# Opening loads on two DMA queues: x on GpSimd's, the weights of block 0 on SP's

## The chip, the cores and the metric

The kernel runs on one core of a Trainium2 chip. The metric is the device time of one execution in microseconds (us). The core has TensorE (PE in the profile; PEld is its weight load), VectorE (DVE), ScalarE (ACT), GpSimd (POOL) and SyncE (SP). SP and GpSimd each have a DMA queue here; both are served by the core's 16 DMA engines.

## What is computed

One decoder block on x of 256 tokens by 1024 channels, float32: an RMS norm, one input projection to 9216 columns, two branches (a gated linear recurrence and a block-sparse attention), a gated sum, an output projection and a SwiGLU network. Cut to its frame:

```python
h = rmsnorm(x, attn_norm_g[l])
proj = h @ w_in[l]
hq, hf, hi, hg, aq, ak, av, gl = jnp.split(proj, IN_SPLITS, axis=-1)
y_hg = hgrn2_mix(hq, hf, hi, hg, lb_all[l], hg_out_norm_g[l]) @ w_branch_hg[l]
...
merged = gates[:, :, 0, :] * y_hg + gates[:, :, 1, :] * y_at
x = x + merged @ w_out[l]
h2 = rmsnorm(x, ffn_norm_g[l])
x = x + (jax.nn.silu(h2 @ w_ffn_gate[l]) * (h2 @ w_ffn_up[l])) @ w_ffn_down[l]
```

## The kernel before

Every matrix product runs on TensorE in a two-part number format: a float32 operand is split into a rounded high part and the low rest, and a product takes three matmuls (high by high, high by low, low by high). The split of weights is the helper `split` (lines 55 and 56): ACT makes the high part, DVE the low part.

The kernel is written with a tile framework that keeps each engine's work in an order chosen at build time by a planner with modelled durations, and sets the waits. An engine executes its own instructions strictly in that order.

The opening, lines 116 to 155, computes block 0 of the projection, that is the first 512 columns of `hi` (columns 2048 to 2559 of `w_in`), into the two PSUM banks `V0`. The 1024 channels are 8 k-tiles of 128. For a k-tile it needs a slice of x (transposed, 128 partitions by 256 tokens, tile `xTr`) and a slice of the weights (128 by 512, tile `raw`, shown as `wraw`). ACT multiplies x by the norm gain, a column of the small tile `vec`, and makes the high part `x_hi` (line 143); DVE makes the low part `x_lo` (line 144); both go to the tiles `XT`, which all later blocks of the projection use as well. ACT and DVE split the weights, and PE makes six matmuls per k-tile, three for each half of the tokens (lines 152 to 154).

The loads come in pieces of k-tiles 0, 1, 2 and 3, 4 and 5, 6 and 7. A k-tile of x is 128 KB, one of the weights 256 KB; `vec` is 17.5 KB. All are issued by SP, in the order x piece, weights piece, and `vec` after the first x piece:

```python
for n in pieces:
    ks = slice(k0, k0 + n)
    xs = slice(4 * g + k0, 4 * g + k0 + n)
    nc.sync.dma_start(xTr[:, xs, :], xT[:, xs, :])
    if g == 0 and k0 == 0:
        nc.sync.dma_start(vec, vecs)
    nc.sync.dma_start(raw[:, ks, :], ...)
```

The weight tiles come from a pool of three buffers (`wp`), shared with all later blocks. After block 0 the kernel starts `feat_block` for the forget gate (F0, matmuls on lines 98, 99 and 101), whose weights SP loads through `load_w` (line 64), then the load of x by tokens (`xtok`, line 206) and the next blocks. GpSimd makes constants at the start (`ones_r`, the identity `ident`, the masks: lines 158 to 172); its first DMA is that of line 258, followed by three loads of a bias table from device memory (line 264).

Of the kernel before, what the change touches and what calls it, by code (L numbers as in the profile page):

```python
# [14 lines left out]
P = 128  # L15
# [12 lines left out]
def tile_hgrn2_moba_block(ctx: ExitStack, tc: tile.TileContext, xm, xT, vecs, table, onehot,  # L28
                          w_in, w_hg, w_at, w_out, w_gate, w_up, w_down, out):
    nc = tc.nc  # L30
# [7 lines left out]
    def pw(name="pw"):  # L38
        return psum.tile([P, 512], F32, name=name, tag="pw", bufs=4)
# [11 lines left out]
    def part(pair, k, m):  # L51
        return pair[k // 4][:, k % 4, m, :]

    def split(src, hi, lo):
        nc.scalar.copy(hi, src)  # L55
        nc.vector.tensor_sub(lo, src, hi.bitcast(F32))  # L56
# [68 lines left out]
    xTr = big.tile([P, KT, S], F32, name="xTr", tag="T1")  # L125
    XT = [big.tile([P, 4, 2, S], F32R, name=f"XT{i}", tag=("XH", "XL")[i]) for i in range(2)]
    V = big.tile([P, 2, D], F32, name="V", tag="T6")
    V0 = [pw(), pw()]
    for g, pieces in enumerate(((1, 1, 2), (2, 2))):
        raw = wp.tile([P, 4, 512], F32, name="wraw")  # L130
        wh = wp.tile([P, 4, 512], F32R, name="whi")
        wl = wp.tile([P, 4, 512], F32R, name="wlo")
        k0 = 0
        for n in pieces:
            ks = slice(k0, k0 + n)
            xs = slice(4 * g + k0, 4 * g + k0 + n)
            nc.sync.dma_start(xTr[:, xs, :], xT[:, xs, :])
            if g == 0 and k0 == 0:
                nc.sync.dma_start(vec, vecs)
            nc.sync.dma_start(raw[:, ks, :], w_in[xs.start * P:xs.stop * P, 2048:2560].rearrange("(k p) c -> p k c", p=P))  # L140
            for kt in range(xs.start, xs.stop):
                x_hi, x_lo = part(XT, kt, 0), part(XT, kt, 1)
                nc.scalar.mul(x_hi, xTr[:, kt, :], vec[:, kt:kt + 1])
                nc.vector.scalar_tensor_tensor(x_lo, xTr[:, kt, :], vec[:, kt:kt + 1], x_hi.bitcast(F32),
                                               op0=OP.mult, op1=OP.subtract)
                if kt == xs.start:
                    split(raw[:, ks, :], wh[:, ks, :], wl[:, ks, :])
            for i in range(k0, k0 + n):
                kt = 4 * g + i
                for tb in range(2):  # L150
                    ts = slice(tb * P, (tb + 1) * P)
                    nc.tensor.matmul(V0[tb], part(XT, kt, 0)[:, ts], wh[:, i, :], start=(kt == 0), stop=False)
                    nc.tensor.matmul(V0[tb], part(XT, kt, 1)[:, ts], wh[:, i, :], start=False, stop=False)
                    nc.tensor.matmul(V0[tb], part(XT, kt, 0)[:, ts], wl[:, i, :], start=False, stop=(kt == KT - 1))
            k0 += n
# [7 lines left out]
    for j in range(7):  # L163
        c = 1 << j
# [54 lines left out]
    def put_tok(dst, ps, half):  # L219
        for tb in range(2):  # L220
            nc.scalar.mul(dst[:, tb, half * 512:(half + 1) * 512], ps[tb], rx[:, tb:tb + 1])

    put_tok(V, V0, 0)

# [313 lines left out]
    for half in range(2):  # L538
# [9 lines left out]
        for j in range(2):  # L548
            ks = slice(half * 4 + 2 * j, half * 4 + 2 * j + 2)
# [10 lines left out]
    for half in range(2):  # L560
        ps = tok_block(w_out, half * 512, M)
        for tb in range(2):
            xs = x2[:, tb, half * 512:(half + 1) * 512]
# [112 lines left out]
```

## Time and profile before

| | |
|---|---|
| median of 3 runs | 513.78 us (513.46 to 514.15) |
| the profiled execution, its time | 513.5 us |
| the profiled execution, its span (first to last instruction) | 511.4 us |
| PE busy | 502.2 us, 98% of the span |
| DVE, ACT, POOL busy | 69%, 57%, 5% of the span |
| granted TensorE clock, mean | 1.000 |

The span leaves out 2.1 us around the program. Matmul durations overlap their neighbours, so a busy PE is not one at its peak; how far apart matmuls start tells its pace. In a timeline row the bracket at the end is the idle time of that engine just before the row, and what ended it. SPq is SP's DMA queue: a row of it is the issue of a DMA, not the transfer.

### The profile page before, as it was taken

The page shows a single profiled execution, that of the slowest core. Times are in us where ns is not written, and L with a number is a line of the kernel's source. Part 1 is how long each engine was busy: PE and PEld are TensorE (multiplying, and loading weights), DVE is VectorE, ACT ScalarE, POOL GpSimd, SP SyncE. Part 2 cuts the span into 40 slices and gives each one's busy share as a digit, 9 for nine tenths or more (in the row PEclk, how much of TensorE's full clock was granted, in tenths as well). Part 3 has the DMA queues.
Part 4 walks back from the last instruction along what each step waited for, and adds up shares of the span by engine and source line. Part 5 has one row for each costly group of instructions (what it writes and reads, how often), then busy time and mean ns, then how long its engine had stood idle before and what let it go on. Part 6 is the DMA issues. An engine that isn't in the chain of part 4 may idle for free.

```text
span 511.4 us, 6690 instructions
## 1 busy us (share of the span) xinstructions
PE 502.2 (98%) x2674; PEld 427.5 (84%) x2674; DVE 350.9 (69%) x406; ACT 291.8 (57%) x447; POOL 25.4 (5%) x42
## 2 busy tenths in 40 slices
PE   6999999999999999999999999999999999999996
PEld 5878878788888888988888888888888888888885
DVE  4769998977597663297667777767665646657372
ACT  5597538776639644975554464665634535444250
POOL 8002340000000000000000000000000000000000
PEclk9999999999999999999999999999999999999999
DMA  7956955725422743256665456555655565553522
GB/s 234 390 197 182 347 178 168 243 82 166 164 84 82 247 142 106 83 171 242 190 213 173 166 181 229 165 164 172 208 198 164 186 226 165 177 193 86 181 105 82
DMA packets 43806, 91.20 MB, mean 178 GB/s; under 512 B 1880, under 2 KB 4472, under 8 KB 43776
## 3 DMA queue, kind: packets, MB, share of 16 engines
q1 hardware_dynamic: 43040, 88.14, 51.8%
q0 software_dynamic: 736, 2.65, 1.7%
q8 instruction: 21, 0.34, 0.3%
q14 instruction: 9, 0.07, 0.0%
HBM read 89.70 MB, written 1.07 MB: 178 GB/s over the span
## 4 chain that ended last, share of the span: by engine, by line
PE 86%; DVE 6%; ACT 3%; DMA 1%; POOL 1%; issue 1%; SPq 0%; DVEq 0%; POOLq 0%
PE pw L99 30%; PE pw L98 13%; PE pw L83 6%; PE pw L81 6%; PE pw L82 6%; PE acc L598 4%; PE acc L596 4%; PE acc L597 4%; DVE wlo L56 3%; PE ph L320 2%; PE pw L101 2%; ACT whi L55 2%; DMA wraw<-w_in 1%; POOL qk L295 1%; PE pa L437 1%
## 5 line engine op out<-in xcount | busy, mean ns | idle before, releaser
L56 DVE TENSOR_TENSOR wlo<-wraw,whi 128x2048 fp32r<-128x2048 f32 (+2 forms) x88 | 190.8, 2169 | 105.4 <-ACT whi L55 105.0
L55 ACT CAST whi<-wraw 128x2048 fp32r<-128x2048 f32 (+2 forms) x88 | 156.0, 1774 | 104.4 <-issue 29.5
L99 PE MATMUL pw<-x2T,whi 128*128 128x512 f32 x352 | 121.8, 398 | 0.0
L99 PE MATMUL pw<-XT,whi 128*128 128x512 f32 x256 | 89.6, 399 | 0.0
L98 PE MATMUL pw<-x2T,wlo 128*128 128x256 f32 x308 | 86.6, 281 | 0.0
L99 PEld LDWEIGHTS pw<-x2T,whi 128*128 128x128 f32 x352 | 63.5, 188 | 12.3
L98 PE MATMUL pw<-XT,wlo 128*128 128x256 f32 x224 | 62.8, 281 | 0.0
L98 PEld LDWEIGHTS pw<-x2T,wlo 128*128 128x128 f32 x308 | 58.3, 189 | 1.8
L81 PE MATMUL pw<-whi,XT 128*128 128x512 f32 x144 | 56.9, 395 | 0.8 <-DVE Q L111 0.8
L82 PE MATMUL pw<-wlo,XT 128*128 128x512 f32 x144 | 56.8, 394 | 0.0
L83 PE MATMUL pw<-whi,XT 128*128 128x512 f32 x144 | 56.5, 392 | 0.0
L99 PEld LDWEIGHTS pw<-XT,whi 128*128 128x128 f32 x256 | 46.5, 188 | 9.9 <-ACT Fg L110 0.4
L98 PEld LDWEIGHTS pw<-XT,wlo 128*128 128x128 f32 x224 | 42.4, 189 | 1.4
L596 PE MATMUL acc<-whi,hT 128*128 128x512 f32 x88 | 34.3, 390 | 0.0
L598 PE MATMUL acc<-whi,hT 128*128 128x512 f32 x88 | 34.3, 390 | 0.0
L597 PE MATMUL acc<-wlo,hT 128*128 128x512 f32 x88 | 34.3, 389 | 0.0
L81 PEld LDWEIGHTS pw<-whi,XT 128*128 128x128 f32 x144 | 27.1, 188 | 6.5 <-DVE Q L111 1.1
L83 PEld LDWEIGHTS pw<-whi,XT 128*128 128x128 f32 x144 | 27.0, 188 | 5.6
L82 PEld LDWEIGHTS pw<-wlo,XT 128*128 128x128 f32 x144 | 27.1, 188 | 5.5 <-DVE wlo L56 0.3
L110 ACT COPY fl<-pw 128x256 f32<-128x256 f32 x38 | 14.0, 370 | 24.9 <-PE pw L99 24.9
L99 PE MATMUL pw<-aT,whi 128*128 128x512 f32 x64 | 22.3, 397 | 0.0
L99 PE MATMUL pw<-oT,whi 128*128 128x512 f32 x64 | 22.3, 397 | 0.0
(209 smaller groups left out, 708.4 us busy)
## 6 DMA issues: line engine op xcount, KB each, us to landing
wraw<-w_in SPq DMA_DIRECT2D x32, 1024.0 KB, 5.2
wraw<-w_down SPq DMA_DIRECT2D x11, 1024.0 KB, 4.8
wraw<-w_gate SPq DMA_DIRECT2D x10, 1024.0 KB, 5.0
wraw<-w_up SPq DMA_DIRECT2D x10, 1024.0 KB, 5.0
wraw<-w_at SPq DMA_DIRECT2D x4, 1024.0 KB, 4.9
wraw<-w_hg SPq DMA_DIRECT2D x4, 1024.0 KB, 5.0
wraw<-w_out SPq DMA_DIRECT2D x4, 1024.0 KB, 5.0
wraw<-w_in SPq DMA_DIRECT2D x7, 512.0 KB, 8.8
```

Of the source, the lines that this page charges most:

```text
L55: nc.scalar.copy(hi, src)
L56: nc.vector.tensor_sub(lo, src, hi.bitcast(F32))
L81: nc.tensor.matmul(ps[tb], part(act, kt, 0)[:, ts], wh, start=(kt == 0), stop=False)
L82: nc.tensor.matmul(ps[tb], part(act, kt, 0)[:, ts], wl, start=False, stop=False)
L83: nc.tensor.matmul(ps[tb], part(act, kt, 1)[:, ts], wh, start=False, stop=(kt == KT - 1))
L98: nc.tensor.matmul(ps[ct][:, 0:S], lo[:, i, cs], part(act, kt, 0), start=False, stop=False)
L99: nc.tensor.matmul(ps[ct], hi[:, i, cs], both, start=(kt == 0), stop=(kt == KT - 1))
L101: nc.tensor.matmul(ps[ct][:, 0:S], lo[:, i, cs], part(act, kt, 0), start=False, stop=False)
L110: nc.scalar.copy(dst, hi)
L596: nc.tensor.matmul(acc[tb][half], act[:, j, 0, ts], hi[:, i, cs], start=st, stop=False)
L597: nc.tensor.matmul(acc[tb][half], act[:, j, 0, ts], lo[:, i, cs], start=False, stop=False)
L598: nc.tensor.matmul(acc[tb][half], act[:, j, 1, ts], hi[:, i, cs], start=False, stop=en)
```

## The change

SP issues x of k-tile 0 first. GpSimd's queue gets the other k-tiles of x in three DMAs (k-tile 1, 2 and 3, 4 to 7), ahead of its constants. In the loop SP issues only the weights, and `vec` after the weights of k-tile 0.

```diff
     V0 = [pw(), pw()]
+    nc.sync.dma_start(xTr[:, 0:1, :], xT[:, 0:1, :])
+    for k0, k1 in ((1, 2), (2, 4), (4, 8)):
+        nc.gpsimd.dma_start(xTr[:, k0:k1, :], xT[:, k0:k1, :])
     for g, pieces in enumerate(((1, 1, 2), (2, 2))):
         raw = wp.tile([P, 4, 512], F32, name="wraw")
...
         for n in pieces:
             ks = slice(k0, k0 + n)
             xs = slice(4 * g + k0, 4 * g + k0 + n)
-            nc.sync.dma_start(xTr[:, xs, :], xT[:, xs, :])
+            nc.sync.dma_start(raw[:, ks, :], w_in[xs.start * P:xs.stop * P, 2048:2560].rearrange("(k p) c -> p k c", p=P))
             if g == 0 and k0 == 0:
                 nc.sync.dma_start(vec, vecs)
-            nc.sync.dma_start(raw[:, ks, :], w_in[xs.start * P:xs.stop * P, 2048:2560].rearrange("(k p) c -> p k c", p=P))
```

## Rows read from the trace of the kernel before

**Rows 1.** The page: span, and median landing of the 1024 KB loads of w_in.

```profile
span 511.4 us, 6690 instructions
...
wraw<-w_in SPq DMA_DIRECT2D x32, 1024.0 KB, 5.2
```

**Rows 2.** Busy time by stage, sum over 13 to 490 us (four stages).

```profile
sum 477.00, PE 475.84 PEld 406.48 DVE 335.13 ACT 281.77 POOL 14.50; mean PE 118.96 PEld 101.62 DVE 83.78 ACT 70.44 POOL 3.63
```

**Rows 3.** Timeline of PE in block 0: start, duration, line; the last is F0's first.

```profile
5.32 0.79 PE L152 MATMUL pw<-whi,XT 128*128 128x512 f32 x1 [0.42 <-ACT whi L55]
...
9.33 0.40 PE L154 MATMUL pw<-wlo,XT 128*128 128x512 f32 x1
12.14 0.49 PE L152 MATMUL pw<-whi,XT 128*128 128x512 f32 x1 [2.41 <-ACT whi L55]
...
20.83 0.39 PE L99 MATMUL pw<-XT,whi 128*128 128x512 f32 x1
```

**Rows 4.** Timeline of ACT: the split of the weights of k-tiles 2 and 3.

```profile
11.04 1.04 ACT L55 CAST whi<-wraw 128x1024 fp32r<-128x1024 f32 x1 [1.13 <-DMA wraw<-w_in]
```

**Rows 5.** Timeline of SP's queue, 0 to 7 us: start and duration of each issue.

```profile
0.81 0.38 SPq L137 DMA_DIRECT2D xTr<-xT  x1
1.25 0.42 SPq L139 DMA_DIRECT2D vec<-vecs  x1
1.71 0.42 SPq L140 DMA_DIRECT2D wraw<-w_in  x1
...
2.65 0.43 SPq L140 DMA_DIRECT2D wraw<-w_in  x1
...
3.60 0.43 SPq L140 DMA_DIRECT2D wraw<-w_in  x1
...
4.59 0.43 SPq L140 DMA_DIRECT2D wraw<-w_in  x1
5.07 1.19 SPq L137 DMA_DIRECT2D xTr<-xT  x1
6.30 0.80 SPq L140 DMA_DIRECT2D wraw<-w_in  x1
```

**Rows 6.** DMA issues at 3.60, 4.59 and 6.30: size, us to landing.

```profile
wraw<-w_in SPq DMA_DIRECT2D x1, 512.0 KB, 7.4
...
wraw<-w_in SPq DMA_DIRECT2D x1, 512.0 KB, 8.8
...
wraw<-w_in SPq DMA_DIRECT2D x1, 512.0 KB, 9.2
```

**Rows 7.** Windows: stretch, busy times (x instructions), clock, share of DMA engines, GB/s.

```profile
3.00:5.00 2.00, 1.90 (x9) 1.61 (x8) 1.47 (x8) 1.04 (x3) 2.00 (x5) 1.00 0.87 268
5.00:6.50 1.50, 1.18 (x3) 0.99 (x4) 1.20 (x3) 0.68 (x2) 1.50 (x4) 1.00 0.60 113
6.50:8.00 1.50, 1.40 (x5) 0.76 (x3) 0.12 (x1) 0.62 (x1) 1.50 (x6) 1.00 0.95 270
8.00:11.00 3.00, 1.69 (x6) 0.97 (x6) 1.57 (x3) 0.91 (x2) 3.00 (x11) 1.00 0.99 335
...
13.00:20.00 7.00, 6.93 (x31) 5.44 (x30) 6.33 (x9) 5.44 (x8) 0.00 (x0) 1.00 1.05 395
```

**Rows 8.** Timeline of POOL: the issue of its first load of the bias table.

```profile
48.97 0.94 POOL L264 DMA_DIRECT2D Bx<-line_d  x1 [1.72 <-DMA line_d<-line]
```

**Rows 9.** DMA issues: a small one of each queue, us to landing.

```profile
line_d<-line POOLq DMA_DIRECT2D x1, 24.0 KB, 2.1
vec<-vecs SPq DMA_DIRECT2D x1, 17.5 KB, 2.1
```

**Rows 10.** Timeline of SP's queue, 54 to 58 us: two loads of weights, merged.

```profile
54.64 3.24 SPq L64 DMA_DIRECT2D wraw<-w_in  x2
```

**Rows 11.** DMA: packets by queue from 55.8 to 58.4; landing of the issue at 54.64.

```profile
q0 software_dynamic: 199, 0.75, 102.2%
...
wraw<-w_in SPq DMA_DIRECT2D x1, 1024.0 KB, 8.1
```

## The prediction

> **What bounds the kernel now.** I read the page first: the span is 511.4 us [rows 1]. The windows by stage come next: from 13 to 490 us TensorE is busy for 475.84 of 477.00 us [rows 2], so it is the bound there, idle for 1.2 us in all. A microsecond won or lost before 13 us therefore comes out at the end almost whole. That leaves the opening, and the timeline of PE shows it [rows 3]: the first matmul of block 0 starts at 5.32, k-tiles 0 and 1 (six matmuls each) are done at 9.33 + 0.40 = 9.73, and the next matmul, of k-tile 2, starts at 12.14. The hole of 2.41 us is ended by ACT's split of the weights. ACT in turn starts that split at 11.04 after waiting 1.13 us for the DMA of the weights of k-tiles 2 and 3 [rows 4]. So the one thing that sets the end, as far as this change reaches, is the landing of that 512 KB piece, which I call w23 (likewise w0, w1, w45, w67, and x0, x1, x23, x47 for the pieces of x).
>
> The queue of SP shows w23 issued at 3.60, as the seventh DMA, about 0.47 us after each other [rows 5]; it landed 7.4 us later, at 11.0 [rows 6]. Seven microseconds are far more than an issue costs, so the reader should ask whether w23 waits for SP or for the DMA engines. The windows answer that: the engines are 87% busy from 3 to 5 us, 60% from 5 to 6.5, 95% to 8, 99% to 11 [rows 7]. Mostly they are full, at a poor 113 to 335 GB/s against 395 later. SP also runs into its own backlog: the issue at 5.07 takes 1.19 us instead of 0.43 [rows 5].
>
> **The change part by part.** *SP loses four x issues* (x1, x23 and the two halves of x47), 0.47 us each. Weights go out earlier: w0 at about 1.25 instead of 1.71, w1 at 2.18 instead of 2.65, w23 at 2.65 instead of 3.60, as vec now comes third. Were the issue the limit, w23 would land 0.95 us earlier. With backlogged engines it is worth only what the engines are short of work.
>
> *vec goes behind w0.* It is issued 0.46 us later and its packets stand behind 256 KB. ACT's first product scales x0 by a column of vec, so the first matmul may slip from 5.32 by up to about a microsecond. It is hidden by the hole of 2.41 us before k-tile 2; with the hole gone it would cost its full length.
>
> *GpSimd gains three issues in front of its constants* (ones_r, ident, the masks). One of its later issues takes 0.94 us [rows 8]; at that pace x1, x23 and x47 go out at about 0.8, 1.7 and 2.6 (SP's first goes out at 0.81 [rows 5]), and the constants start some 2.7 us later. Their first user is far behind in the program (the identity for the row scale, after all of block 0 and the first F block), so this costs nothing. The lag after an issue is the same on both queues: 24 KB from GpSimd land after 2.1 us, 17.5 KB from SP after 2.1 us [rows 9].
>
> *x changes its place among the bytes.* K-tile 2 needs x0, vec, w0, x1, w1, x23 and w23: 128 + 17.5 + 256 + 128 + 256 + 256 + 512 = 1553.5 KB, before and after; that is what SP's queue had in front of 11.0, in this order. So the two queues save no byte of what the hole waits for. New is that x47, 512 KB that only k-tiles 4 to 7 need, can come in between: it is issued at about 2.6, w23 at 2.65, a tie. What it costs: w45 landed at 4.59 + 8.8 = 13.4 [rows 5, 6], 768 KB behind w23 (x45 and itself), so the last bytes of a piece came at 768 / 2.4 = 320 KB/us. All of x47 in front costs 512 / 320 = 1.6 us, none of it nothing. I take the half, +0.8, since the two are issued together.
>
> *Against it stands the idle time of the engines.* From 3 to 11 us they were without work for 2 x 0.13 + 1.5 x 0.40 + 1.5 x 0.05 + 3 x 0.01 = 0.97 us [rows 7]. A second queue can fill some of it, above all the 40% of the stretch where SP's own issue was stuck. Bounds: nothing and 0.97; I take half, -0.5. Whether an engine really works on both queues side by side is seen once in the trace. At 54.64 SP issues 1024 KB of weights while GpSimd's table loads run [rows 10]; from 55.8 to 58.4 every packet is of GpSimd's queue, and the weights land after 8.1 us [rows 11], where such a load takes 5.2 in the median [rows 1]. So the queue that came later got nothing until the other was through: order of arrival, or one queue until it is dry, and no sharing.
>
> The Trainium skill says otherwise (DMA: Bandwidth & Descriptors, Queues, rings and completion order): an engine goes round between the queues, a packet at a time. The same page (Issuing engines are not separate DMA queues) holds that issuing from several engines saves only the sequencer's issue time, since all run on the same 16 engines. By the first, x47 would be mixed into w1 and w23 and nearly all of it stand before the end of w23: +1.6 us instead of +0.8. The row above does not bear the turn-taking out; that nothing but issue time is saved agrees with engines that are 95 to 99% busy.
>
> *Sum:* +0.8 - 0.5 = +0.3 us. The profiled execution took 513.5 us in all, 0.28 below the median of the three runs, 513.78. I add to the median: 514.1 us.
>
> **The rivals.** A measurement of this kernel can tell a change of about 0.2%, 1.03 us, from none.
>
> *Forecast: the hole stays, shifted by less than 1.03 us either way* (512.8 to 514.8). For it: the same 1553.5 KB on nearly full engines. Chance 0.43.
>
> *x in front, slower.* All 512 KB of x47 come before w23, by turn-taking between queues (the rule of the page above), or because GpSimd issues sooner, or because ACT's and DVE's order now has the products of later k-tiles before the split of w23, so that an early x is waited for. Nothing of the idle time is filled. It decides as soon as over 330 KB of x47 are in front (1.03 x 320). Price +1.6 us, 515.4; at the 270 GB/s of 6.5 to 8 us [rows 7], 264 KB/us, it is 1.9 us, 515.7. Against it: w23 leaves SP no later than x47 leaves GpSimd. Chance 0.25.
>
> *Starved x, slower by much.* If an engine stays on one queue until it is dry, SP's weights, never dry, shut out GpSimd's x. Ahead of x1 would be x0, vec, all of w0 to w67 and the first 1024 KB of the next block, 3217.5 KB. Before, 3089.5 KB had landed with w67 at 6.30 + 9.2 = 15.5 [rows 5, 6]; at 395 GB/s [rows 7], 386 KB/us, x1 would land near 15.8 and k-tile 1 start near 16.6 (0.8 for the product of x1, my estimate). Six k-tiles took 20.83 - 12.14 = 8.7 us [rows 3], seven take 10.1: block 0 ends at 26.7 instead of 20.83, +5.9 us, 519.7. For it: the rows of 54.64 to 58.4. Against it: x1 and x23 are issued when the engines have little yet. Chance 0.08.
>
> *Issue-bound, faster.* The landing of w23 follows its issue, since SP's stuck queue, and not the engines, made the 60% stretch. Then w23 gains its 0.95 us of issue and up to 0.97 us of filled idle time: -0.95 to -1.9 in all, and never over the hole, 2.41. About 512.3; it counts as faster from 1.03 on. For it: the issue of 1.19 us at 5.07. Against it: 99% busy from 8 to 11. Chance 0.24.
>
> **How the numbers follow.** Likeliest is the forecast, 514.1, alone from 512.8 to 514.8. Faster 0.24 (issue-bound), same 0.43, slower 0.25 + 0.08 = 0.33. The range leaves out the starved case and the outer part of the faster one: from 513.78 - 1.6 = 512.2 to 515.7 and 0.3 for an order on ACT that waits for an early x, 516.0.
>
> **What would show it.** In the profile after, the hole before k-tile 2 on PE: start at 12.1 plus or minus 1 (forecast), 13.7 or later (x in front), 10.2 to 11 (issue-bound), near 17 with x as the releaser (starved). ACT's wait before the split of w23 should name the weights' DMA; if it names x, GpSimd's queue is the late one. The DMA share from 5 to 6.5 should rise above 0.60 if idle time is filled. The first matmul of block 0 should start at 5.3 to 6.3, without effect on the end. From 13 us on the busy times should be those of before. I am wrong if a queue gives way in a manner that no row here shows, or if the shorter queue of SP makes the early packets themselves faster.

## The result and the profile after

The changed kernel takes 516.78 us in the median (516.17 to 517.22, six runs), the kernel before 513.89 in the same session (513.46 to 514.96, six runs). The ratio is 1.0061, 95% interval [1.0045, 1.0077]: slower by 0.6%, about 3.1 us (2.9 by the medians), and outside the range given. Here and below the ratio of a run is not the quotient of the two medians; where the executions of a kernel scatter, the two differ a little. The profiled execution took 517.22 us, the longest of the six, with a span of 515.3, so it stands 0.4 us above its median, and 3.9 us of span above the one of before [rows 1].

The opening first. Timeline of PE in block 0 (the answer to [rows 3]):

```profile
5.71 1.22 PE L154 MATMUL pw<-whi,XT 128*128 128x512 f32 x2 [0.80 <-ACT XT L145]
...
8.01 0.63 PE L156 MATMUL pw<-wlo,XT 128*128 128x512 f32 x1
11.53 0.80 PE L154 MATMUL pw<-whi,XT 128*128 128x512 f32 x1 [2.89 <-ACT whi L55]
12.12 0.63 PE L155 MATMUL pw<-whi,XT 128*128 128x512 f32 x1
12.55 0.70 PE L156 MATMUL pw<-wlo,XT 128*128 128x512 f32 x1
...
17.03 0.40 PE L155 MATMUL pw<-whi,XT 128*128 128x512 f32 x1
17.26 0.40 PE L156 MATMUL pw<-wlo,XT 128*128 128x512 f32 x1
...
23.64 0.39 PE L99 MATMUL pw<-XT,whi 128*128 128x512 f32 x1
```

The hole of 2.89 us is there again, but it stands one k-tile earlier: only the six matmuls of k-tile 0 are done before it. Behind it the matmuls start 0.43 us apart, and 0.23 us from about 17 us on. Block 0 ends at 23.64 instead of 20.83. Timeline of ACT, and below it the DMA issues of x23, w1, x47 and w23 in this order (size, us to landing; issued at 2.04, 2.18, 2.59 and 2.66):

```profile
10.85 0.62 ACT L55 CAST whi<-wraw 128x512 fp32r<-128x512 f32 x1 [4.80 <-DMA wraw<-w_in]
...
12.87 1.05 ACT L55 CAST whi<-wraw 128x1024 fp32r<-128x1024 f32 x1 [0.19 <-DMA wraw<-w_in]
```

```profile
xTr<-xT POOLq DMA_DIRECT2D x1, 256.0 KB, 7.8
wraw<-w_in SPq DMA_DIRECT2D x1, 256.0 KB, 8.7
...
xTr<-xT POOLq DMA_DIRECT2D x1, 512.0 KB, 9.3
wraw<-w_in SPq DMA_DIRECT2D x1, 512.0 KB, 10.2
```

The split that ends the hole waited 4.80 us for w1, which landed at 2.18 + 8.7 = 10.9. w23 landed at 2.66 + 10.2 = 12.86, 1.8 us later than before (11.02). Windows of 3 to 13 us and of 13 to 490 us (the answer to [rows 7] and [rows 2]):

```profile
3.00:5.00 2.00, 1.91 (x9) 1.61 (x8) 0.00 (x0) 0.62 (x1) 1.98 (x6) 1.00 0.69 216
5.00:6.50 1.50, 0.79 (x2) 0.64 (x3) 1.42 (x5) 0.91 (x2) 1.50 (x3) 1.00 0.56 137
6.50:8.00 1.50, 1.50 (x5) 1.14 (x4) 0.21 (x1) 0.00 (x0) 1.50 (x4) 1.00 0.86 281
8.00:11.00 3.00, 0.64 (x2) 0.00 (x0) 0.00 (x0) 0.15 (x1) 3.00 (x12) 1.00 1.02 395
11.00:13.00 2.00, 1.48 (x3) 1.00 (x4) 1.50 (x3) 1.81 (x5) 2.00 (x8) 1.00 1.06 401
...
13.00:490.00 477.00, 474.51 (x2553) 405.66 (x2552) 332.83 (x385) 279.95 (x432) 14.03 (x12) 1.00 0.54 180
```

The engines idle more than before, not less: 2 x 0.31 + 1.5 x 0.44 + 1.5 x 0.14 = 1.49 us against 0.97. And something is lost after 13 us too, where the prediction saw nothing to look for. It is the stretch around 70 us. Timeline of the kernel after, by engine (the bias-table product on PE, GpSimd's two flips of the table, ACT, DVE, and PE's first matmul of the next V block):

```profile
46.65 0.59 PE L256 MATMUL pa<-oh,tb_sb 32*8 32x256 f32 x2
...
61.48 1.20 POOL L271 COPY B<-Bx 128x1024 f32<-128x1024 f32 x1 [4.62 <-DMA Bx<-line_d]
65.58 1.07 POOL L271 COPY B<-Bx 128x1024 f32<-128x1024 f32 x1 [2.90 <-DMA Bx<-line_d]
...
66.69 1.14 ACT L316 COPY KP<-K 128x1024 f32<-128x1024 f32 x1 [5.48 <-DVE F L337]
67.72 1.92 ACT L55 CAST whi<-wraw 128x2048 fp32r<-128x2048 f32 x1
...
69.67 2.29 DVE L56 TENSOR_TENSOR wlo<-wraw,whi 128x2048 fp32r<-128x2048 f32 x1 [2.97 <-ACT whi L55]
71.88 1.08 DVE L111 TENSOR_TENSOR Q<-pw,Q 128x256 f32<-128x256 f32 x3
...
72.35 0.50 PE L81 MATMUL pw<-whi,XT 128*128 128x512 f32 x1 [2.11 <-DVE Q L111]
```

The same instructions in the timeline of the kernel before:

```profile
33.04 0.59 PE L254 MATMUL pa<-oh,tb_sb 32*8 32x256 f32 x2
...
60.01 1.58 POOL L269 COPY B<-Bx 128x1024 f32<-128x1024 f32 x1 [1.67 <-DMA Bx<-line_d]
...
61.62 1.14 ACT L314 COPY KP<-K 128x1024 f32<-128x1024 f32 x1 [2.88 <-POOL B L269]
62.83 1.92 ACT L55 CAST whi<-wraw 128x2048 fp32r<-128x2048 f32 x1
...
68.80 0.50 PE L81 MATMUL pw<-whi,XT 128*128 128x512 f32 x1 [0.79 <-DVE Q L111]
```

Read it as a chain. The planner put the bias-table product 13.6 us later, behind one more block of matmuls, though the diff does not touch it. With it came the store of the line, the table loads and GpSimd's flips. The second flip reads a buffer of tag T15, and the copy `KP` on ACT needs that buffer. On ACT a split of weights stands behind `KP`; DVE's half of the split follows, and behind that, on DVE, stand the additions for Q that free PE's banks. PE stands for 2.11 us instead of 0.79. The row of `KP` names DVE's F as releaser; F and the flip ended within 0.05 us of each other (64.75 + 1.95 and 65.58 + 1.07), so the name alone settles nothing.

In the profiled pair the loss of 3.9 us of span is 2.81 at the end of block 0, 0.74 more up to the first V matmul (72.35 - 23.64 = 48.71 against 68.80 - 20.83 = 47.97), and some 0.35 after that.

### The profile page after: what moved, and what is told of

The parts are those of the page before. It is cut to its first block, busy times and chain, and to the rows that moved or that the text cites. A ratio compares the mean times of both kernels' runs of the same rounds, so it can differ in the third digit from the quotient of the medians.

```text
span 515.3 us, 6691 instructions
## 1 busy us (share of the span) xinstructions
PE 503.7 (98%) x2674; PEld 429.2 (83%) x2674; DVE 349.4 (68%) x406; ACT 291.7 (57%) x447; POOL 25.9 (5%) x45
## 3 DMA queue, kind: packets, MB, share of 16 engines
HBM read 89.70 MB, written 1.07 MB: 176 GB/s over the span
## 4 chain that ended last, share of the span: by engine, by line
PE 87%; DVE 5%; ACT 3%; DMA 2%; POOL 1%; issue 1%; SPq 0%; DVEq 0%; POOLq 0%
PE pw L99 30%; PE pw L98 14%; PE pw L83 6%; PE pw L81 6%; PE pw L82 6%; PE acc L600 4%; PE acc L598 4%; PE acc L599 4%; PE ph L322 2%; DVE wlo L56 2%; ACT whi L55 2%; PE pw L101 2%; DMA wraw<-w_in 2%; POOL qk L297 1%; PE pa L439 1%
## 6 DMA issues: line engine op xcount, KB each, us to landing
wraw<-w_in SPq DMA_DIRECT2D x7, 512.0 KB, 11.1
```

## The experiments

Twelve kernels, five rounds each, in three sessions, where the kernel before had 513.3, 513.34 and 513.41 us. The theories were first about the opening alone.

**Vec first on SP's queue.**

```diff
+            if g == 0 and k0 == 0:
+                nc.sync.dma_start(vec, vecs)
             nc.sync.dma_start(raw[:, ks, :], w_in[...])
-            if g == 0 and k0 == 0:
-                nc.sync.dma_start(vec, vecs)
```

> Changed kernel, with vec issued before the weights of k-tile 0 again. In the changed kernel block 0 ends 2.81 us later than before (23.64 against 20.83). Theory 'late pieces': 1.8 us of it are w23, which lands at 12.86 instead of 11.02, because w1 and w23 stand behind x23 and x47 on most DMA engines; 1.0 us is PE, which runs at half pace (0.43 us from one matmul of 512 columns to the next) up to 16.5 us. By it the first matmul comes back to about 5.3, w1 still lands near 10.8, and the gain is at most the 1.0 us of the pace: 515.8 to 516.8 us. Rival 'pace': the landings hardly matter, all of the loss is the half pace, which comes of the longer gap before the first matmul (0.80 instead of 0.42 us); full pace from about 7.3 us on would bring block 0 back to about 21 us: 513.9 to 514.4 us.

Measured: 518.06 us, ratio 1.0075 [1.0048, 1.0102]; neither theory has it so. The first matmul waits for w0's split at 6.33 instead. w1 landed after 6.7 us and w23 after 8.9, 2.0 and 1.3 us sooner than in the profile after, block 0 ended at 22.10, and the whole was no shorter. The split of w23 did not gain its 1.3 us: in ACT's order of this build it stands behind two products that wait for x47, as the timeline of ACT shows:

```profile
11.41 0.91 ACT L145 ACTIVATE XT<-xTr,vec 128x256 fp32r<-128x256 f32 x2 [1.49 <-DMA xTr<-xT]
12.22 1.03 ACT L55 CAST whi<-wraw 128x1024 fp32r<-128x1024 f32 x1
```

The hole behind the copy `KP`, before PE's first V matmul, is 2.2 us here too.

**x47 off GpSimd's queue,** issued by SP behind w23.

```diff
-    for k0, k1 in ((1, 2), (2, 4), (4, 8)):
+    for k0, k1 in ((1, 2), (2, 4)):
...
+            if g == 1 and k0 == 0:
+                nc.sync.dma_start(xTr[:, 4:8, :], xT[:, 4:8, :])
             nc.sync.dma_start(raw[:, ks, :], w_in[...])
```

> Changed kernel, but GpSimd carries only x1 and x23; SP issues x47 itself, after w23. 'Late pieces': with x47 out of the way w1 lands by about 8 and w23 by about 11.0 to 11.3 us, as before, so most of the loss goes: 513.8 to 514.6 us. Rival 'slow queue': transfers that GpSimd issues are slow by themselves (packets of 0.3 to 1.2 us are nearly all its own in the changed kernel), and x1 and x23 alone keep w1 late, beyond 9.5 us: 515.5 us or more.

Measured: 517.55 us, 1.006 [1.0037, 1.0083]. w23 landed 8.5 us after 2.65, at 11.1, so x47 in front is indeed what delayed w23 (by 1.7 us against the profile after); w1 still took 7.6 us, as the rival 'slow queue' has it, the hole stayed before k-tile 1 (2.40 us), and block 0 ended at 21.41. Yet the median did not move; the profiled execution, at 515.89 us, lies 1.7 us below it and does not show all of the loss. A place where time went, in the timelines of ACT and PE of this kernel:

```profile
59.69 1.09 ACT L318 COPY KP<-K 128x1024 f32<-128x1024 f32 x1 [5.14 <-POOL B L273]
...
61.56 0.50 PE L99 MATMUL pw<-XT,whi 128*128 128x512 f32 x1 [2.19 <-DVE Q L111]
```

Here the flip is the releaser without doubt, 5.14 us of ACT's time.

**Eight filler matmuls behind k-tile 0's,** into a bank that nobody reads, against the half pace.

```diff
+            if g == 0 and k0 == 0:
+                for _ in range(8):
+                    nc.tensor.matmul(warm, part(XT, 0, 0)[:, 0:P], wh[:, 0, :], start=True, stop=True)
             k0 += n
```

> Changed kernel, with eight extra matmuls of 512 columns on k-tile 0's data into the warm-up bank (their result is not used) in the time in which PE waits for w1. Nothing changes for the DMA. 'Late pieces': PE is at full pace when w1 comes, block 0 ends at about 22.6 instead of 23.64, and 1.0 us is given back: about 515.8 us; w1 and w23 land at 10.8 and 12.9 as in the changed kernel. Rival 'pace': all of the loss goes, 513.9 to 514.4 us.

Measured: 516.86 us, 1.0064 [1.0041, 1.0086]. The hole shrank to 1.53 us, but from 11.69 on k-tile 1's matmuls were some 0.4 us apart all the same, and block 0 ended at 22.92. No gain.

**x on ACT's DMA queue** instead of GpSimd's.

```diff
-        nc.gpsimd.dma_start(xTr[:, k0:k1, :], xT[:, k0:k1, :])
+        nc.scalar.dma_start(xTr[:, k0:k1, :], xT[:, k0:k1, :])
```

> Changed kernel, with the three x loads on ACT's DMA queue instead of GpSimd's (issued at about 0.8, 2.8 and 3.2 us, since the planner puts two of them behind ACT's table load). 'Slow queue': a queue of the same kind as SP's does not hold w1 up, w1 lands by about 7.5 and w23 by 11 us: 514.3 us or less. 'Late pieces': x23 and x47 still stand in front of w23 on most engines, w23 lands at 12 us or later: 515.2 to 517 us.

Measured: 516.01 us, 1.0053 [1.0036, 1.0069]. This is the run that broke the theories of the opening: w23 landed at 10.5, block 0 ended at 20.78, as in the kernel before, and 2.7 us were lost none the less. Its timelines (GpSimd, ACT, PE) and, last, the window of 69 to 73 us:

```profile
63.04 1.04 POOL L271 COPY B<-Bx 128x1024 f32<-128x1024 f32 x1 [1.22 <-DMA Bx<-line_d]
...
64.11 1.13 ACT L316 COPY KP<-K 128x1024 f32<-128x1024 f32 x1 [5.88 <-POOL B L271]
...
69.76 0.80 PE L81 MATMUL pw<-whi,XT 128*128 128x512 f32 x1 [2.49 <-DVE Q L111]
70.36 0.63 PE L82 MATMUL pw<-wlo,XT 128*128 128x512 f32 x1
70.78 0.63 PE L83 MATMUL pw<-whi,XT 128*128 128x512 f32 x1
```

```profile
69.00:73.00 4.00, 3.24 (x8) 2.60 (x9) 3.93 (x8) 0.93 (x1) 0.82 (x1) 0.57 0.59 173
```

The hole behind `KP` is 2.49 us, and after it the granted clock is 0.57 for the stretch, nearly the lower of the two levels (1.2 of 2.4 GHz), with matmuls 0.43 us apart. So the theory became: most of the loss is the late bias chain. Four kernels moved that chain.

**The bias-table product ahead of block F0,** in the kernel after, in the kernel before, and in the one with x on ACT's queue; and, in the kernel before, behind the first Q block instead. The lines from `oh` to `line_d` move in one piece (in the last also the flips). Where the expectations say "ahead of block 0", the edit puts the product behind block 0 and ahead of F0; in the first kernel it runs at 22.27 us.

```diff
+    oh = big.tile([NB, S], F32, name="oh", tag="T11")
...
+    nc.gpsimd.dma_start(line_d, line)
     F0 = feat_block(w_in, 1024, XT, cut=2)
```

> The changed kernel with the bias-table product (its loads, the product, the copies and the store of the line) written ahead of block 0, so that TensorE has it as its 50th matmul and GpSimd's flips come early. Theory A, the late bias chain: the changed kernel lost 2.9 us, of which the late flips and the KP copy on ScalarE behind them gave some 1.5 to 2 at 66 to 72 us; with the chain early that hole is 1 us or less, and the whole is 514.3 to 515.3 (ratio to the kernel before 1.001 to 1.004); block 0 still ends 1.5 to 3 us late. Theory B, the opening alone: what is lost at block 0's end stays lost and nothing later matters, 516.3 to 517.3 (ratio 1.0055 to 1.0075), the same as the changed kernel.

> The kernel before, with its own opening loads, and the bias-table product moved ahead of block 0. Theory A: the hole of 0.8 us that the kernel before has at 67.6 us, where the matmuls wait for a Q that stands behind the KP copy, goes, so 512.3 to 513.2 (0.998 to 0.9995, or no change that can be measured). Theory B: order after block 0 is worth nothing, 513.3 to 513.9 (1.000).

> x on ScalarE's queue and the bias-table product ahead of block 0. With x on that queue alone block 0 ended no later than in the kernel before (20.78 against 20.83 us) and yet the whole was 0.5% longer. Theory A: the rest was the late bias chain, so that this one equals the kernel before or is a little faster, 512.5 to 513.7 (0.998 to 1.0005). Theory B, something else that comes from the second queue or from the new order (a TensorE clock at half for longer, for one): 515 to 516 (1.003 to 1.005) as with x on that queue alone.

> The kernel before, its opening untouched, with the bias-table product written behind the first block of Q, one block later than the changed kernel has it. Theory A: the flips end past 65 us, the KP copy on ScalarE and the loads and splits behind it are late, and the whole is slower by 1 to 3 us with an unchanged block 0 (514.5 to 516.5, 1.002 to 1.006). Theory B: no change, 513.3 to 513.9 (0.999 to 1.001).

Measured: in the kernel after 513.91 us, 1.0013 [1.0000, 1.0027]: most of the loss is gone with the opening untouched. In the kernel before 513.14, 1.0004 [0.9989, 1.0020], no gain. With ACT's queue 514.83, 1.0048 [1.0028, 1.0068], a miss for the theory. Late in the kernel before 515.74, 1.0052 [1.0037, 1.0068]: the same size of loss as the change's, with the opening of before. (Its block 0 was not unchanged, though: it ended at 22.42 in the profiled execution, which lies 1.1 us above the median. From the first V matmul on, its span is 2.5 us longer than in the kernel before.) What stands in for the hole at 70 us, in the timelines of PE of the second, the third and the fourth kernel:

```profile
36.66 0.39 PE L101 MATMUL pw<-XT,wlo 128*128 128x256 f32 x1 [0.88 <-DVE wlo L56]
```

```profile
48.69 0.47 PE L99 MATMUL pw<-XT,whi 128*128 128x512 f32 x1 [3.06 <-ACT whi L55]
```

```profile
88.04 0.50 PE L82 MATMUL pw<-wlo,XT 128*128 128x512 f32 x1 [1.46 <-DVE wlo L56]
```

Each build has its own order. Three of the four orders have a hole of their own on ACT's and DVE's splits, at 36.7, 48.7 or 88.0 us (the last one also 1.26 us at 96.2); the first has none behind block 0. So these four show that order after block 0 is worth 2 to 3 us, and that moving a whole chain is too blunt to say which wait costs them. The next edit touches one buffer.

**The second flip on tag T9 instead of T15,** in the kernel after, with x on ACT's queue, and in the kernel before; and, as the fourth, with ACT's queue and vec ahead of w0 (the edits shown above, together).

```diff
-    flip(B1[:, :, P:S], 384 + 128, "T15")
+    flip(B1[:, :, P:S], 384 + 128, "T9")
```

In the first two the order of PE, DVE and GpSimd is the same as without the edit; on ACT only `KP` moves, ahead of two splits.

> The changed kernel with one buffer moved: GpSimd's second flip reads from a buffer of tag T9 in place of T15, so that the KP copy on ScalarE no longer waits for it. The order of TensorE, VectorE and GpSimd stays as in the changed kernel; on ScalarE the KP copy alone stands elsewhere. Theory A, the buffer: the hole of 2.1 us before the first V matmul (72.35 in the changed kernel) falls to 0.8 or less, and of the 2.9 us loss 1.3 to 2.1 come back: 514.5 to 515.5 (ratio to the kernel before 1.002 to 1.004); what is left is the opening's. Theory B, the later weights' splits are late by themselves because everything is 2.8 us later: the hole stays at 2 us, 516.3 to 517.3 (1.0055 to 1.0075).

> x on ScalarE's queue and the second flip on T9. With x on that queue block 0 ended at 20.78 us (20.83 in the kernel before), and the hole of 2.5 us behind the KP copy made it slower. Theory A: with that wait gone the hole is 0.8 us or less, and the whole equals the kernel before or beats it by up to 0.8 us, 512.5 to 513.7 (0.9985 to 1.0005). Theory B, the hole has another cause or another hole opens, as with the bias product ahead of block 0 (3.1 us at 45 us there): 515 to 516 (1.003 to 1.005).

> The kernel before with the second flip on T9; ScalarE's KP copy then stands some 3 us earlier. Theory A: the hole of 0.79 us at 68.8 us, behind the same copy, goes, 512.5 to 513.1 (0.9985 to 0.9995). Theory B: that hole is the weights' own, and nothing changes, 513.2 to 513.7 (0.9995 to 1.0005).

> As the one with x on ScalarE's queue and the flip on T9, with vec ahead of w0 on SP's queue. In the two runs with x on that queue the first matmul waited until 8.4 to 8.9 us, behind vec, which landed at 7.8. Theory A: the first matmul starts at 6.5 to 7.5, block 0 still ends with what w23's landing of 10.5 allows, 19.8 to 20.8, and the whole is 512 to 513.4 (0.997 to 1.000). Theory B, vec early is worth nothing because w1 or w23 sets the end: within 0.3 us of the version without it.

Measured: the kernel after with this one buffer moved takes 513.54 us, ratio 0.9998 [0.9986, 1.0010]. The whole loss is gone. Timelines of ACT, GpSimd and PE of this kernel:

```profile
50.56 1.15 ACT L316 COPY KP<-K 128x1024 f32<-128x1024 f32 x1
...
64.07 1.05 POOL L271 COPY B<-Bx 128x1024 f32<-128x1024 f32 x1 [2.94 <-DMA Bx<-line_d]
...
22.08 0.39 PE L99 MATMUL pw<-XT,whi 128*128 128x512 f32 x1
...
68.53 0.40 PE L81 MATMUL pw<-whi,XT 128*128 128x512 f32 x1
```

`KP` runs at 50.56 and waits for nothing, the second flip is late as in the kernel after and nobody waits for it, and the V matmul has no hole before it. From F0 to V it is 68.53 - 22.08 = 46.45 us, where the kernel before needs 47.97. With x on ACT's queue the edit gives 512.00 us, 0.9981 [0.9967, 0.9994], where that kernel had 1.0053 [1.0036, 1.0069] without it: a little more than expected. The kernel before gains nothing that can be told: 513.05, 0.9995 [0.9979, 1.0010]; its hole of 0.79 went to 0.44. The last one, ACT's queue with vec first, has the lowest median: 511.39 us, 0.9961 [0.9947, 0.9974], a version that beats both kernels; from the one without vec first it is not told apart, since the intervals overlap. Its expectation missed two numbers: the whole came out below 512, and the first matmul came at 7.94, behind w0 now. Its w23 landed 7.1 us after 2.65, at 9.75, and block 0 ended at 20.55. Timeline of PE, and windows of 5 to 6.5 and 8 to 11 us:

```profile
7.94 0.50 PE L154 MATMUL pw<-whi,XT 128*128 128x512 f32 x1 [3.03 <-ACT whi L55]
...
20.55 0.39 PE L99 MATMUL pw<-XT,whi 128*128 128x512 f32 x1
```

```profile
5.00:6.50 1.50, 0.00 (x0) 0.00 (x0) 1.06 (x5) 0.51 (x1) 1.50 (x5) 1.00 0.98 381
...
8.00:11.00 3.00, 3.00 (x9) 2.41 (x10) 2.32 (x5) 2.57 (x5) 3.00 (x9) 0.67 1.05 397
```

## Why the prediction was wrong

**The step that decided: "From 13 us on the busy times should be those of before".** The prediction's sum, +0.8 - 0.5, has no term for anything behind block 0. But the order of instructions is planned from modelled durations of the whole program, and a change of the opening changed the order 30 us later. The T9 run takes away the wait that came of it and leaves the order of PE, DVE and GpSimd as it is: 1.0061 against 0.9998, 0.63% or 3.2 us, with about 1 us either way by the two intervals. In the profiles, from F0's first matmul to the end of the span, which leaves block 0 out, the kernel after takes 515.3 - 23.64 = 491.7 us and the T9 run 510.9 - 22.08 = 488.8: 2.9 us. With x on ACT's queue the same edit is worth 0.72% (1.0053 to 0.9981). Of the 2.9 us, 2.11 are the hole. The half pace that follows the hole in some executions (0.57 for 4 us with ACT's queue) may be part of the rest; the runs do not divide it. Why the planner moved the product was not tried.

**What the opening cost by itself.** One pair of traces does not price it, because block 0's end scatters with one and the same opening. Its last matmul starts at 20.44, 20.60, 21.93 and 22.19 us in the four traces with the opening of before, and at 21.86, 21.95 and 23.41 in three with the change's; the profiled pair, 20.60 and 23.41, lies far apart among these. The T9 runs with GpSimd's and with ACT's queue have the same order after block 0, but for the place of one matmul. They differ by 513.54 - 512.00 = 1.5 us in the medians and by 0.17%, 0.9 us, in the ratios, and the second ends block 0 where the kernel before does (20.89 and 20.83). So GpSimd's opening costs about 0.9 to 1.5 us against ACT's. The new order, once rid of the wait, gives about as much back: 512.00 - 513.41 = -1.4 by the medians, 0.19% or -1.0 by the ratio; from F0's first matmul to the end of the span it takes 488.4 us (509.3 - 20.89, ACT's queue) or 488.8 where the order of before takes 511.4 - 20.83 = 490.6. The three terms (opening, new order, wait) add up to the measured loss because each is a difference to the next run, so their sum proves nothing by itself. That the T9 run takes as long as the kernel before is luck: the opening's loss and the new order's gain happen to cancel.

**"The one thing that sets the end is the landing of w23", with k-tiles 0 and 1 covered by the hole.** Wrong for w1. It was issued 0.47 us earlier and landed at 10.9 (10.2 to 10.3 in three more traces with this queue for x and vec behind w0) instead of 2.65 + 4.7 = 7.4, so the cover of 2.41 us was gone and the hole moved one k-tile forward. Bytes in front do not make all of that: with x47 out of the way it still landed at 9.8, and the 256 KB of x23 are 0.8 us at the prediction's 320 KB/us. When a piece has slack its own landing must be priced too, if other transfers can hold it up. GpSimd's three issues, 1.80 us from 1.33 on, were harmless as said. vec behind w0 moved the first matmul little, as said (5.71 instead of 5.32), but its place was not free: with vec first again w1 landed at 8.9 and w23 at 11.6, and with ACT's queue w23 came at 9.7 instead of 10.5. Why is open.

**x47 in front, +0.8.** Mis-sized: w23 came 1.8 us later in the profiled pair (12.86 for 11.02). It landed at 10.8 to 11.4 in the four traces with the opening of before, at 12.3 in three more traces with x on GpSimd's queue and vec behind w0, and at 11.1 with x47 behind w23. So x47 in front was worth some 1.2 to 1.7 us. That is near the rival "x in front" with its price of 1.6 to 1.9, though not its total.

**Idle time filled, -0.5.** Wrong sign on GpSimd's queue: 0.5 us more idle time. In the run with vec first the engines idled for only 2 x 0.03 + 1.5 x 0.03 + 1.5 x 0.09 = 0.24 us, and w23 still landed later than before (11.6), so a busy share is not a rate. On ACT's queue the stretch of 5 to 6.5 us did fill (0.96 to 1.02). Whether SP's stuck issue is what left it short of work is not shown. The issue-bound rival falls: w23 was issued 0.94 us earlier and landed 1.8 us later.

**One queue until it is dry, no sharing.** Not so here, and the starved x did not come: x23 landed before w1. Packets by queue from 5 to 6.5 us in the kernel after (queue, packets, MB, share of the engines; q0 is GpSimd's):

```profile
q0 software_dynamic: 27, 0.09, 31.3%
q1 hardware_dynamic: 62, 0.12, 24.7%
```

Both queues are served at once. The Trainium skill (DMA: Bandwidth & Descriptors, Queues, rings and completion order) has the engines go round between the queues, and x47 in front of w23 agrees with that; so do the packets on ACT's queue, shown at the end, 154 of one queue to 156 of the other, while the 27 to 62 here are not one to one. It was named as a rule that would give +1.6, and set aside for one row at 54 us; that row does not hold for this stretch. (The sum of the starved rival leaves out the 128 KB of x1 itself, 0.3 us, which changes nothing here.)

**The bound of 98% busy.** A TensorE that idles 1.2 us in 477 has little slack to hide a new wait, which the prediction read right: the hole that the order opened came out at the end, and the 1.3 us that PE is less busy from 13 to 490 us (474.51 for 475.84) are about the growth of this one hole (2.11 for 0.79).

## What to carry to other kernels

Where the order is planned from modelled times, compare the order of the new build with the old on every engine before pricing anything: an edit of 1 MB of loads at 2 us moved an unrelated product by 14 us, and the wait behind it cost more than the new opening did. A hole that appears far from the edit is best tested by taking away one dependency (another buffer tag) with the rest of the order unchanged; moving whole chains opened new holes in three of four tries. Which engine issues the second queue matters: with x on GpSimd's the weights of k-tiles 2 and 3 came some 1.3 us later than before, with x on ACT's 0.5 us sooner. But not even there did block 0 end clearly sooner (20.89, and 20.55 with vec first, for 20.83), since its first matmul came at 8.4 and 7.9; what the fastest kernel won lies behind block 0, in the new order without the wait (509.0 - 20.55 = 488.5 us for 490.6). And a single trace does not price an opening: with one and the same opening block 0's end differed by 1.6 to 1.8 us.

## What the runs showed of the hardware

As a second queue beside SP's, GpSimd's did not raise the rate of the opening, and ACT's did. From 5 to 6.5 us the engines moved 113 to 165 GB/s with SP's queue alone (four traces), 134 to 187 with x on GpSimd's (six) and 351 to 381 with x on ACT's (four). The busy shares, in the same order, are 0.57 to 0.66, 0.43 to 0.71 and 0.96 to 1.02; only the trace with GpSimd's queue and vec first does not fit, with 0.97 at 168 GB/s. With x on ACT's queue 1553.5 + 512 = 2065.5 KB had landed with w23 at 10.5 us, where the kernel before had 1553.5 at 11.0. The 512 KB more are an estimated 1.3 us at 386 KB/us, so what was won there, 1.3 + 0.5 = 1.8 us by this estimate, is more than the 0.95 us by which w23 is issued earlier; the prediction's second rule, that nothing but issue time is saved, is not borne out. Packets by queue for the same stretch with x on ACT's queue and the flip on T9 (q10 is ACT's):

```profile
q10 hardware_dynamic: 154, 0.48, 82.5%
q1 hardware_dynamic: 156, 0.04, 13.4%
```

A packet of x took 0.825 x 16 x 1.5 / 154 = 0.13 us there, and 0.313 x 16 x 1.5 / 27 = 0.28 us on GpSimd's queue in the kernel after, for about 3 KB each (0.48 MB / 154, 0.09 MB / 27); by the same reckoning it is 0.12 to 0.15 us in the other three traces with ACT's queue and 0.18 to 0.45 in the other five with GpSimd's. Why is open.

In the kernel after, the window shows a granted clock of 1.00 from 11 to 13 us, where matmuls start 0.43 us apart, the pace that goes with 0.57 in the run with ACT's queue. So here the two readings do not agree, and the distance of the starts is what sets the time. After idle times of like length the pace differed too: at 72.35 us, after 2.11 us, matmuls were at once 0.23 to 0.33 us apart (below), and at 69.76 in the run with ACT's queue, after 2.49 us, 0.43. What tells the two apart was not tried.

```profile
72.68 0.39 PE L82 MATMUL pw<-wlo,XT 128*128 128x512 f32 x1
72.91 0.40 PE L83 MATMUL pw<-whi,XT 128*128 128x512 f32 x1
```
